# Output and FFN left factors built from rows kept in SBUF at written units, and the gate pair's weight sums ordered behind the softmax heads

## The chip, the core and the metric

The kernel runs on one core of a Trainium2 chip. TensorE (PE) multiplies matrices into PSUM, its weight loads (PEld) overlap the multiplications; VectorE (DVE), ScalarE (ACT) and GpSimd (POOL) do the elementwise work; SyncE (SP) issues nearly all DMA transfers between DRAM and SBUF. Each engine takes its instructions in the order in which the compiled program has them; semaphores order them across engines. The metric is the device time of one execution in microseconds, here the median of several timed runs; less is better.

## What is computed

One decoder layer on 512 tokens of width 2048, all in float32 (`reference`, cut):

```python
h = rms_norm(x, norm1_g[l])
proj = h @ w_in[l]
qa, ka, va, ra, ga, qb, kb, vb = jnp.split(proj, split_points, axis=-1)
log_g = jax.nn.log_sigmoid(ga @ gla_gate_w2[l] + gla_gate_b[l]) / GLA_GATE_TAU
out_a = gla_mixer(qa, ka, va, ra, log_g, onorm_g)      # 4 heads, ends with  * silu(ra)
out_b = dilated_mixer(rms_norm(qb), rms_norm(kb), vb, rel_bias)   # 8 softmax heads
mix = jnp.concatenate([out_a, out_b], axis=-1)
x = x + mix @ w_out[l]
h2 = rms_norm(x, norm2_g[l])
x = x + (jax.nn.silu(h2 @ w_gate[l]) * (h2 @ w_up[l])) @ w_down[l]
```

Nearly all arithmetic is in five matrix products with `w_in`, `w_out`, `w_gate`, `w_up` and `w_down` (2048 to 5632 wide).

## The kernel before

**Products.** Each large product is done with one level of Strassen's scheme (the Winograd form): the left factor (activations, transposed) and the weights are cut into quarters, and seven products P1 to P7 of sums of quarters replace eight. A left sum is called A11, S1, S2, S4, S3, A12 or A22 and belongs to P1, P5, P6, P3, P7, P2 or P4 in that order, which is the order in which they run. Float32 accuracy is had by splitting every factor into a high and a low part: the high part is a cast on ScalarE, the low part a subtraction on VectorE, and three of the four products of parts are taken.

**Pairs and units.** Class `Pair` stands for two column blocks of 512 columns that share a left factor. `stream` walks through the pairs. A pair has 7 products times 4 groups of rows: 28 units, and a unit is one weight quarter of 128x1024 elements with 12 matmuls (line 358): eight with the weight's high part, four with its low part. For unit k the loop does in this order: the high part of the weight of unit k+1 on ScalarE (line 331), the weight sum of unit k+2 on VectorE (`total`, which calls `Pair.source`, line 256; P5, P6, P7 and P4 need one), the low part of unit k+1 on VectorE (line 335), eight matmuls, then `p.step()`, then four matmuls. P5 subtracts quarter a from b, P6 a from d, P7 b from d, P4 a from c, each time into the second one's buffer.

**Left factors.** Class `Operand` holds the split left sums. `split` makes one from a row tile: a cast on ScalarE (line 161), a subtraction of 512 columns on VectorE (line 162), into a buffer of the pool `apool` (28 buffers). The left factor of the output projection (`opm`) has rows of the softmax heads as its upper half (`mix_d[4]` to `mix_d[7]`) and rows of the GLA heads as its lower half (`mix_d[0]` to `mix_d[3]`); that of the FFN (`opn`) is made of the normed output (`xn_d`). In the kernel before, all these rows are stored to DRAM when they have been turned (`transposed_store`, TensorE transposes at line 1019, ScalarE copies at lines 1027 and 1030, store at line 1034) and fetched again whenever a sum needs them (`part`, line 1073, and `fetch_part`, line 1107).

**Order.** `step` first runs what was put off with `later(units, ...)` and then takes one step of the first generator in `background`; `rate` and `paced` say at which units a step is taken. In the gate pair (columns 2048 and 2560 of the input projection, the last pair over `opx`) 0.72 steps a unit are taken: `dil_heads(4)` and `dil_heads(6)`, two softmax heads at a time in eight steps each, then `early_job` for A11 and S3 of `opm`; what isn't made when the output pair begins is made there at once (`finish`). During the output pair `late_jobs` makes the rest, one sum and split per unit, with loads one item ahead. For the FFN's left factor `operand_jobs` builds groups 0 and 1 during the second output pair, and `early_job` and `late_jobs` groups 2 and 3 at the beginning of the first FFN pair.

A step of a softmax head (`scores`) is: one score matmul (line 904), an add with a running minimum on VectorE (line 907), an exponential on ScalarE (line 910), a reciprocal (line 913) and a multiplication on VectorE (line 914).

The first pair alone is ordered by hand (`PLAN`). For the rest, a list scheduler of the framework orders each engine's instructions when the program is compiled; an instruction whose inputs it holds to be ready may be put far ahead of its place in the text. `tc.issue_after(ins)` adds an edge: what is traced inside the block comes after `ins` on that engine.

Of the kernel before, what the change touches and what calls it, by code (L numbers as in the profile page):

```python
# [18 lines left out]
P = 128  # L19
# [6 lines left out]
NB = 640  # L26
PRODUCTS = ("P1", "P5", "P6", "P3", "P7", "P2", "P4")
# [69 lines left out]
def block_kernel(ctx: ExitStack, tc: tile.TileContext, ins, out):  # L97
# [138 lines left out]
    class Pair:  # L236


        def __init__(self, op, rows, w1, w2, final, step, scale=None, before=None):
            self.op, self.rows, self.w1, self.w2 = op, rows, w1, w2  # L240
            self.final, self.step, self.scale, self.before = final, step, scale, before
            self.q, self.dst, self.held = {}, {}, {}

# [6 lines left out]
        def source(self, prod, g):  # L250

            if prod in SINGLE:
                return self.quarter(SINGLE[prod], g)
            one, two = SUMS_OF[prod]
            src = self.quarter(two, g)
            nc.vector.tensor_tensor(src, self.quarter(one, g), src, op=ALU.subtract)  # L256
            return src
# [608 lines left out]
    def dil_head(h, lane):  # L866
# [34 lines left out]
        def scores(b):  # L901
# [5 lines left out]
            nc.vector.tensor_tensor_reduce(  # L907
                lg[:, :n], lp[:, :n], tb[:, 512 - n :], -1.0, 3.0e38, ALU.add, ALU.min, st[:, 0:1]
            )
# [4 lines left out]
            nc.vector.tensor_scalar(lg[:, :n], lg[:, :n], st[:, 3:4], None, op0=ALU.mult)  # L914
# [51 lines left out]
    def in_turn(*gens):  # L966
        for g in gens:
            yield from g


    def heads_norm(t):
# [4 lines left out]
        for h in range(4):  # L976
# [35 lines left out]
    def transposed_store(tiles, half, dsts, gains=None, spare=None):  # L1012

        for b in range(2):
# [7 lines left out]
            if spare is None:  # L1022
                d = work(("oT", "PT")[b], (P, 2, 256))
            else:
                d = spare[:, b]
            if gains is None:
                nc.scalar.copy(d, bk)
            else:
                for jj in range(2):
# [3 lines left out]
                    )  # L1033
            store(dsts[b][half], d)
            done.add((id(dsts[b]), half))

    def final_gate(half, which, tiles, acc_):
# [11 lines left out]
        for m in range(2):  # L1049
# [27 lines left out]

    def early_job(op, wanted, flip):
        h0, h1 = (1, 0) if flip else (0, 1)
        return op.early([(g, part(top, h0), part(top, h1)) for g, top in wanted])  # L1080
# [31 lines left out]
    def late_jobs(op, groups, tops, bots, flip):  # L1112

        h0, h1 = (1, 0) if flip else (0, 1)
        tt = nc.vector.tensor_tensor
        sums = {}

        def sum_of(name, g, op1):
            def use(t):
                if name == "S1":  # L1120
                    tt(sums[g], t, sums[g], op=ALU.add)
                elif name == "S2":
                    tt(sums[g], sums[g], t, op=ALU.subtract)
                else:
                    tt(sums[g], t, sums[g], op=ALU.subtract)
                op.split(name, g, sums[g])

            return use

        def both(g):  # L1130
            fetch = fetch_part(tops[g], h1)[1]

            def get():
                sums[g] = part(bots[g], h1)()
                return fetch()

            return (id(bots[g]), h1), get

        items = []
        for part_ in groups:  # L1140
            for g in part_:
                items.append((*both(g), sum_of("S1", g, op)))
            for g in part_:
                items.append((*fetch_part(tops[g], h0), sum_of("S2", g, op)))
        groups = [g for part_ in groups for g in part_]
        for g in groups:
            items.append((*fetch_part(bots[g], h0), sum_of("S4", g, op)))
        for name, half in (("A12", h0), ("A22", h1)):
            for g in groups:
                items.append(  # L1150
                    (*fetch_part(bots[g], half), lambda t, name=name, g=g: op.split(name, g, t))
                )
        return staged(items)
# [22 lines left out]
    pair(opx, rows_in, col(2048), col(2560), final_gate, rate((27, 0.72), (1, 0)), row_scale)  # L1176
# [23 lines left out]

    def final_out(second):
        def final(half, which, tiles, acc_):
# [31 lines left out]
    def output_scales(part):  # L1234
# [6 lines left out]
        else:  # L1241
# [7 lines left out]
    pair(opm, rows_mix, ocol(0), ocol(512), final_out(0), paced([1] * 28),  # L1249
         before=lambda: finish(lambda: ("S3", 3) in opm.t))  # L1250
# [181 lines left out]
```

## Time and profile before

| | |
|---|---|
| median of three timed runs | 1965.07 us (1964.33 to 1965.67) |
| profiled execution, device time | 1958.01 us |
| its span, first to last instruction | 1956.1 us |
| TensorE clock granted | 0.999 |
| DMA packets, bytes moved | 158855, 362.52 MB |
| read from and written to DRAM | 298.68 MB and 64.51 MB |

A profile is one execution as the hardware recorded it. Times are in us from the first instruction. A line such as "L335 DVE TENSOR_TENSOR wl<-wa,wh ... x376 | 458.7, 1223" names the source line, the engine, the operation, what it writes and reads, how often, the busy time and the mean duration of one in ns. A bracket such as "[3.91 <-DMA v<-mix_d]" in the timeline is idle time of the engine before an instruction and what ended it. The chain of waits is followed back from the last instruction: at each step to what released it. In windows, each engine has its busy time and, after x, its number of instructions. Matmul ends are modelled, so TensorE shown as busy isn't always at its full pace; counts times the pace tell more.

### The profile page before, as it was taken

What the parts mean: (1) busy time and instruction counts of PE and PEld (TensorE: products, weight loads), DVE (VectorE), ACT (ScalarE), POOL (GpSimd) and SP (SyncE); (2) the same over time, 40 slices, a digit from 0 to 9 for tenths busy, and PEclk for the clock granted to TensorE, in tenths of its full rate; (3) what the DMA queues carried; (4) which work ended last, traced back from release to release, by engine and by line L of the source; (5) the groups of instructions that cost most, each with busy time, mean ns of one, the idle gap of its engine ahead of it and who ended that gap; (6) DMA issues with size and microseconds to landing.
All of it is one profiled execution on the core that took longest, in us unless ns stands there. A gap on an engine that the chain in (4) does not pass through costs nothing.

```text
span 1956.1 us, 25599 instructions
## 1 busy us (share of the span) xinstructions
PE 1918.2 (98%) x9160; PEld 1657.3 (85%) x9160; DVE 1648.0 (84%) x1845; ACT 1088.1 (56%) x1580; POOL 55.2 (3%) x73
## 2 busy tenths in 40 slices
PE   8999999999999999999999999999999999999998
PEld 6788888888878888888888888888888888888887
DVE  7996887768789989878878879879879989989977
ACT  9654554667666665544544545545546646546443
POOL 0000330011000000000000000000000000000000
PEclk9999999999999999999999999999999999999999
DMA  9545555444567584453453453443445865855662
GB/s 355 174 154 206 179 173 171 143 156 162 198 217 241 181 289 148 154 188 141 155 183 135 162 182 120 171 171 124 173 170 176 279 212 182 292 198 180 230 215 76
DMA packets 158855, 362.52 MB, mean 185 GB/s; under 512 B 16438, under 2 KB 43359, under 8 KB 158728
## 3 DMA queue, kind: packets, MB, share of 16 engines
q1 hardware_dynamic: 158584, 360.89, 53.1%
q8 instruction: 71, 1.16, 0.2%
q14 instruction: 56, 0.46, 0.1%
q10 hardware_dynamic: 144, 0.01, 0.0%
HBM read 298.68 MB, written 64.51 MB: 186 GB/s over the span
## 4 chain that ended last, share of the span: by engine, by line
PE 75%; DVE 6%; DMA 3%; issue 2%; ACT 1%; SPq 0%; POOL 0%; DVEq 0%; ACTq 0%
PE acc L358 71%; DVE wl L335 2%; PE bank L1019 1%; DVE wa L256 1%; PE bank L926 1%; PE bank L904 1%; DVE AS L162 1%; PE bank L919 0%; DMA xn_d<-PT 0%; DMA q<-y_d 0%; PE bank L895 0%; DMA q<-in_x 0%; DMA T<-p_d 0%; DMA r<-xn_d 0%; ACT wh L331 0%
## 5 line engine op out<-in xcount | busy, mean ns | idle before, releaser
L358 PE MATMUL acc<-wh,AS 128*128 128x512 f32 x3008 | 712.2, 379 | 0.9 <-DVE AS L162 0.8
L358 PEld LDWEIGHTS acc<-wh,AS 128*128 128x128 f32 x3008 | 568.0, 189 | 82.8 <-DVE AS L162 1.6
L331 ACT CAST wh<-wa 128x1024 fp32r<-128x1024 f32 x376 | 394.3, 1049 | 395.1 <-PE acc L358 365.2
L358 PE MATMUL acc<-wh,AA 128*128 128x512 f32 x2256 | 533.7, 379 | 1.1 <-ACT wh L331 0.9
L335 DVE TENSOR_TENSOR wl<-wa,wh 128x1024 fp32r<-128x1024 f32 x376 | 458.7, 1223 | 74.5 <-ACT wh L331 45.6
L358 PEld LDWEIGHTS acc<-wh,AA 128*128 128x128 f32 x2256 | 426.0, 189 | 62.7 <-ACT wh L331 2.3
L358 PE MATMUL acc<-wl,AS 128*128 128x512 f32 x1504 | 395.3, 385 | 7.6 <-DVE wl L335 7.5
L358 PEld LDWEIGHTS acc<-wl,AS 128*128 128x128 f32 x1504 | 279.2, 189 | 61.0 <-DVE wl L335 20.3
L358 PE MATMUL acc<-wl,AA 128*128 128x512 f32 x1128 | 296.1, 385 | 3.4 <-DVE wl L335 3.3
L358 PEld LDWEIGHTS acc<-wl,AA 128*128 128x128 f32 x1128 | 209.3, 189 | 35.8 <-DVE wl L335 7.5
L331 ACT CAST wh<-wb 128x1024 fp32r<-128x1024 f32 x94 | 98.6, 1049 | 123.8 <-PE acc L358 117.1
L331 ACT CAST wh<-wc 128x1024 fp32r<-128x1024 f32 x94 | 98.4, 1047 | 109.2 <-PE acc L358 106.6
L331 ACT CAST wh<-wd 128x1024 fp32r<-128x1024 f32 x94 | 98.6, 1049 | 103.6 <-PE acc L358 98.5
L335 DVE TENSOR_TENSOR wl<-wc,wh 128x1024 fp32r<-128x1024 f32 x94 | 115.0, 1223 | 41.7 <-ACT wh L331 41.7
L335 DVE TENSOR_TENSOR wl<-wd,wh 128x1024 fp32r<-128x1024 f32 x94 | 114.8, 1223 | 37.8 <-ACT wh L331 28.7
L256 DVE TENSOR_TENSOR wa<-wc,wa 128x1024 f32<-128x1024 f32 x94 | 114.8, 1225 | 35.6 <-DMA wc<-in_w_gate 20.8
L335 DVE TENSOR_TENSOR wl<-wb,wh 128x1024 fp32r<-128x1024 f32 x94 | 114.5, 1221 | 5.3 <-ACT wh L331 4.9
L256 DVE TENSOR_TENSOR wa<-wb,wa 128x1024 f32<-128x1024 f32 x94 | 113.8, 1222 | 1.7 <-DMA wb<-in_w_in 1.0
L256 DVE TENSOR_TENSOR wb<-wd,wb 128x1024 f32<-128x1024 f32 x94 | 114.8, 1223 | 0.4
L256 DVE TENSOR_TENSOR wa<-wd,wa 128x1024 f32<-128x1024 f32 x94 | 113.5, 1223 | 0.1
L298 DVE SCALAR_TENSOR_TENSOR seed<-acc,rs,seed 128x512 f32<-128x512 f32 x96 | 70.5, 747 | 27.6 <-PE acc L358 27.5
L282 ACT ACTIVATE seed<-acc,rs 128x512 f32<-128x512 f32 x96 | 60.8, 682 | 3.1 <-PE acc L358 3.1
(285 smaller groups left out, 1332.2 us busy)
## 6 DMA issues: line engine op xcount, KB each, us to landing
wa<-in_w_gate SPq DMA_DIRECT2D x44, 512.0 KB, 3.4
wb<-in_w_up SPq DMA_DIRECT2D x44, 512.0 KB, 4.0
wd<-in_w_up SPq DMA_DIRECT2D x44, 512.0 KB, 4.1
wc<-in_w_gate SPq DMA_DIRECT2D x44, 512.0 KB, 3.4
wc<-in_w_in SPq DMA_DIRECT2D x28, 512.0 KB, 3.5
wa<-in_w_in SPq DMA_DIRECT2D x24, 512.0 KB, 4.9
wb<-in_w_in SPq DMA_DIRECT2D x24, 512.0 KB, 5.7
wd<-in_w_in SPq DMA_DIRECT2D x24, 512.0 KB, 5.1
```

Source lines behind the costliest of these rows:

```text
L162: nc.vector.tensor_tensor(a[:, :, 1, :], src, a[:, :, 0, :].bitcast(F32), op=ALU.subtract)
L256: nc.vector.tensor_tensor(src, self.quarter(one, g), src, op=ALU.subtract)
L282: nc.scalar.activation(halves(t), unfolded(src[m]), AF.Copy, scale=self.scale(half, m))
L298: nc.vector.scalar_tensor_tensor(halves(seed[m]), unfolded(src[m]), self.scale(half, m), halves(seed[m]), op0=ALU.mult, op1=ALU.add,)
L331: nc.scalar.copy(high[k], sources[k])
L335: nc.vector.tensor_tensor(low[k], sources.pop(k), high[k].bitcast(F32), op=ALU.subtract)
L358: nc.tensor.matmul(p.dst[prod][m], a[:, jj, hl, m * P : (m + 1) * P], folded(w[:, jj, :]), start=fresh and g == 0 and len(terms) == 2 and ...
L904: nc.tensor.matmul(lp[:, :n], qh[:, b * P : (b + 1) * P], kh[:, :n], start=True, stop=True)
L926: nc.tensor.matmul(op, vh[:, k, :], lgs[b][:, k * P : (k + 1) * P], start=(k == 0), stop=(k == b))
L1019: nc.tensor.transpose(bk[:, jj, m * P : (m + 1) * P], tiles[m][:, f : f + P], ident)
```

## The change

- A table `GATE` says at which unit of the gate pair, and `OUT` at which unit of the first output pair, each fetch, sum and split of `opm` is traced (`scripted`, `mixed`). "T.g" fetches both halves of the top row of group g into one buffer; "2.g" makes the sums of S1 and S2. `early_job` and `late_jobs` are gone, and so are the stores of the turned GLA rows: `transposed_store` without `dsts` leaves them in `spare`, and `kept` remembers the tiles.
- For the FFN, the second output pair's turned rows stay in SBUF too (`kept_n`). `kept_job` makes groups 2 and 3 from them, in the order of `KEPT`, one word a step, and waits while a row isn't there. Groups 0 and 1 still go through DRAM. The turn of the last quarter of each output pair is put off by two units instead of three, and the first FFN pair has another list of steps.
- In the gate pair (`hold=True`) each weight sum is traced inside `issue_after` of the latest VectorE instruction of the softmax heads (`recent["head"]`, set at lines 907 and 914).

```diff
+KEPT = "A11.2 A11.3 =S3.2+S3.2 =S3.3+S3.3 =S2.2+=S1.2+S1.2 =S2.3+=S1.3+S1.3 S2.2 S2.3 =S4.2+S4.2 =S4.3+S4.3 A12.2 A12.3 A22.2 A22.3"
+GATE = {
+    9: "T.0 T.1", 11: "A11.0", 12: "S3.0", 13: "A11.1", 14: "S3.1", 16: "T.2", 18: "A11.2", 19: "S3.2",
+    21: "2.0 S1.0", 22: "2.1", 23: "S1.1", 24: "S2.0", 25: "T.3 S2.1", 27: "A11.3",
+}
+OUT = {
+    0: "S3.3", 2: "2.2 S1.2", 3: "2.3 S1.3", 4: "S2.2", 5: "S2.3", 9: "S4.0", 10: "S4.1", 11: "S4.2", 12: "S4.3",
+    17: "A12.0 A12.1", 18: "A12.2", 19: "A12.3", 21: "A22.0", 22: "A22.1", 24: "A22.2", 25: "A22.3",
+}
...
             src = self.quarter(two, g)
-            nc.vector.tensor_tensor(src, self.quarter(one, g), src, op=ALU.subtract)
+            other = self.quarter(one, g)
+            with ExitStack() as behind:
+                if self.hold and "head" in recent:
+                    behind.enter_context(tc.issue_after(recent["head"]))
+                nc.vector.tensor_tensor(src, other, src, op=ALU.subtract)
...
         "qb1": lambda: [
             dil_heads(4),
-            together(dil_heads(6), in_turn(*(early_job(opm, [(g, mix_d[4 + g])], True) for g in range(3)))),
-            early_job(opm, [(3, mix_d[7])], True),
-            late_jobs(opm, ((0, 1), (2, 3)), mix_d[4:], [mix_d[b] for b in order], True),
+            dil_heads(6),
         ],
...
+            if dsts is None:
+                continue
             store(dsts[b][half], d)
...
-        spare = apool.tile([P, 2, 2, 256], F32, name=nm("turned"), tag="A")
-        later(2, lambda: transposed_store(
-            tiles, half, mix_d[2 * which : 2 * which + 2], spare=spare
-        ))
+        def turn():
+            if which == 1:
+                t = apool.tile([P, 2, 2, 256], F32, name=nm("turned"), tag="A")
+                spare = [t[:, 0], t[:, 1]]
+            else:
+                spare = [work(n, (P, 2, 256)) for n in (("qT", "kT"), ("v", "T"))[half]]
+            transposed_store(tiles, half, None, spare=spare)
+            for b in range(2):
+                kept[2 * (which == 0) + b, "r" + str(1 - half)] = spare[b]
+
+        later(2, turn)
...
+    def mixed(name, g):
+        g = int(g)
         tt = nc.vector.tensor_tensor
+        if name == "T":
+            t = apool.tile([P, 2, 2, 256], F32, name=nm("top"), tag="A")
+            for i in range(2):
+                kept[g, "t" + str(i)] = part(mix_d[4 + g], 1 - i)(t[:, i])
+            return
+        t0, t1 = kept[g, "t0"], kept[g, "t1"]
+        if name == "A11":
+            opm.split(name, g, t0)
+        elif name == "S3":
+            tt(t1, t0, t1, op=ALU.subtract)
+            opm.split(name, g, t1)
+        elif name == "2":
+            tt(t1, kept[g, "r1"], t1, op=ALU.subtract)
+            tt(t0, t1, t0, op=ALU.add)
+        elif name == "S1":
+            opm.split(name, g, t0)
+        elif name == "S2":
+            opm.split(name, g, t1)
+        elif name == "S4":
+            tt(t1, kept[g, "r0"], t1, op=ALU.subtract)
+            opm.split(name, g, t1)
+        else:
+            opm.split(name, g, kept[g, "r0" if name == "A12" else "r1"])
...
-    pair(opx, rows_in, col(2048), col(2560), final_gate, rate((27, 0.72), (1, 0)), row_scale)
+    pair(opx, rows_in, col(2048), col(2560), final_gate, scripted(rate((27, 0.72), (1, 0)), GATE), row_scale, hold=True)
...
+    def kept_job(op, kept):
...
+        for word in KEPT.split():
+            for one in word.split("+"):
...
+                while not all(have(n) for n in needs):
+                    yield
...
+            yield
...
             def turn():
-                transposed_store(tiles, tok, dsts, gains)
-                if not second and which == 0 and half == 1:
-                    background.append(operand_jobs(opn, tops, bots, 0, 2))
-                elif second and which == 1 and half == 1:
-                    background.append(early_job(opn, [(g, tops[g]) for g in (2, 3)], False))
-                    background.append(late_jobs(opn, ((2, 3),), tops, bots, False))
-
-            later(3 if which == 0 and half == 1 else 2, turn)
+                if not second:
+                    transposed_store(tiles, tok, dsts, gains)
+                    if which == 0 and half == 1:
+                        background.append(operand_jobs(opn, tops, bots, 0, 2))
+                        background.append(kept_job(opn, kept_n))
+                    return
...
+                transposed_store(tiles, tok, None, gains, spare=kept_n["tr"[which == 0], tok])
+
+            later(2, turn)
...
-    pair(opm, rows_mix, ocol(0), ocol(512), final_out(0), paced([1] * 28),
-         before=lambda: finish(lambda: ("S3", 3) in opm.t))
+    pair(opm, rows_mix, ocol(0), ocol(512), final_out(0), scripted(step, OUT))
...
-    paces = {0: [0, 1, 1, 1, 1, 0, 0, 1, 1] + [0] * 6, 10: [0] * 6}
+    paces = {0: [1, 1, 1, 1, 0, 0, 0, 0, 0, 0, 1, 1, 1, 1, 0, 0, 0, 0], 10: [0] * 6}
     def before_ffn(j):
         if j == 0:
-            finish(lambda: ("S3", 3) in opn.t)
+            finish(lambda: ("A11", 3) in opn.t)
```

More of the change, by code (lines that the diff above doesn't have):

```diff
@@ L26 @@
 NB = 640
+KEPT = "A11.2 A11.3 =S3.2+S3.2 =S3.3+S3.3 =S2.2+=S1.2+S1.2 =S2.3+=S1.3+S1.3 S2.2 S2.3 =S4.2+S4.2 =S4.3+S4.3 A12.2 A12.3 A22.2 A22.3"
+GATE = {
+    9: "T.0 T.1",
+    11: "A11.0",
+    12: "S3.0",
+    13: "A11.1",
+    14: "S3.1",
+    16: "T.2",
+    18: "A11.2",
+    19: "S3.2",
+    21: "2.0 S1.0",
+    22: "2.1",
+    23: "S1.1",
+    24: "S2.0",
+    25: "T.3 S2.1",
+    27: "A11.3",
+}
+OUT = {
+    0: "S3.3",
+    2: "2.2 S1.2",
+    3: "2.3 S1.3",
+    4: "S2.2",
+    5: "S2.3",
+    9: "S4.0",
+    10: "S4.1",
+    11: "S4.2",
+    12: "S4.3",
+    17: "A12.0 A12.1",
+    18: "A12.2",
+    19: "A12.3",
+    21: "A22.0",
+    22: "A22.1",
+    24: "A22.2",
+    25: "A22.3",
+}
 PRODUCTS = ("P1", "P5", "P6", "P3", "P7", "P2", "P4")
@@ L236, in block_kernel, with __init__ @@
     class Pair:
-        def __init__(self, op, rows, w1, w2, final, step, scale=None, before=None):
+        def __init__(self, op, rows, w1, w2, final, step, scale=None, before=None, hold=False):
             self.op, self.rows, self.w1, self.w2 = op, rows, w1, w2
@@ L242, in __init__ @@
             self.q, self.dst, self.held = {}, {}, {}
+            self.hold = hold
         def quarter(self, name, g):
@@ L1110, in fetch_part @@
         return (id(src), half), fetch
-    def late_jobs(op, groups, tops, bots, flip):
-        h0, h1 = (1, 0) if flip else (0, 1)
-        tt = nc.vector.tensor_tensor
[L1116 to L1153, printed above, removed]
@@ new lines, in block_kernel, with scripted, go @@
+    kept = {}
+    def scripted(pace, script):
+        k = [0]
+        def go():
+            pace()
+            for word in script.get(k[0], "").split():
+                mixed(*word.split("."))
+            k[0] += 1
+        return go
+    def mixed(name, g):
+        g = int(g)
+        tt = nc.vector.tensor_tensor
+        if name == "T":
[21 more added lines that the diff above has]
+            opm.split(name, g, kept[g, "r0" if name == "A12" else "r1"])
```

38 lines of the change are left out of this document (31 added, 7 removed).

## The prediction, made before the changed kernel ran

> **What bounds the kernel now.** I read the first part of the page, then the chain of waits, then windows cut where one weight quarter ends and the next begins.
>
> ```profile
> span 1956.1 us, 25599 instructions
> PE 1918.2 (98%) x9160; PEld 1657.3 (85%) x9160; DVE 1648.0 (84%) x1845; ACT 1088.1 (56%) x1580; POOL 55.2 (3%) x73
> ```
>
> TensorE sets the time, and the change adds and removes none of its 9160 matmuls. So the only time to be won is what TensorE spends below its own pace. The pace stands in the chain, where it is alone:
>
> ```profile
> 346.10 5.18 PE acc L358 x24
> 618.07 0.87 PE bank L1019 x8
> ```
>
> One product matmul takes 5.18/24 = 0.216 us and one transpose 0.87/8 = 0.109. A unit (one weight quarter, 12 matmuls) needs 2.59 us. Twenty-eight units are a pair. The change touches the last pair of the input projection (gate pair, from 453 us), the two pairs of the output projection (from 558.54 and from about 642) and the first FFN pair (from about 720). The windows, first of all instructions, then of the product matmuls alone (the count under PEld is exact):
>
> ```profile
> 548.96:558.54 9.58, 8.48 (x40) 6.82 (x38) 9.25 (x13) 6.12 (x10) 0.00 (x0) 1.00 0.86 309
> 558.54:595.46 36.92, 32.56 (x147) 25.46 (x146) 36.92 (x45) 25.15 (x37) 0.00 (x0) 1.00 0.38 129
> 653.36:681.52 28.16, 27.41 (x121) 22.03 (x120) 28.16 (x33) 18.62 (x29) 0.00 (x0) 1.00 0.31 103
> 717.07:757.07 40.00, 34.47 (x161) 28.31 (x160) 35.26 (x45) 26.82 (x45) 0.00 (x0) 1.00 0.58 195
> 756.00:1500.00 744.00, 743.89 (x3523) 650.80 (x3524) 610.55 (x593) 378.53 (x434) 0.00 (x0) 1.00 0.45 159
> ...
> 548.96:558.54 9.58, 8.29 (x38) 6.65 (x36) 1.00 0.86 309
> 558.54:595.46 36.92, 31.32 (x133) 24.08 (x132) 1.00 0.38 129
> 653.36:681.52 28.16, 27.41 (x121) 22.03 (x120) 1.00 0.31 103
> 717.07:757.07 40.00, 33.21 (x145) 26.50 (x144) 1.00 0.58 195
> ```
>
> Columns: length, then busy time and count of PE, PEld, DVE, ACT, POOL, then clock and DMA. Window by window, length minus matmuls times 0.216 minus transposes times 0.109:
>
> - end of the gate pair: 9.58 - 36 x 0.216 - 2 x 0.109 = 1.6 us lost
> - first eleven units of the output projection: 36.92 - 132 x 0.216 - 14 x 0.109 = 6.9 lost, VectorE busy for 36.92 of 36.92
> - 653.36 to 681.52: 28.16 - 120 x 0.216 = 2.3 lost, VectorE full again
> - start of the FFN: 40.00 - 144 x 0.216 - 16 x 0.109 = 7.2 lost, and here VectorE is not full
>
> Together 18.0 us: the ceiling of what the change can give. Behind 756 us TensorE is busy in 743.89 of 744.00, so a stall that is removed earlier isn't found again there.
>
> Two kinds of cause are visible. The first is VectorE having too much to do; the second is VectorE and ScalarE, which work in order, standing before a row that has gone to DRAM and back:
>
> ```profile
> 548.31 0.69 DVE L1121 TENSOR_TENSOR r<-v,r 128x512 f32<-128x512 f32 x1 [3.91 <-DMA v<-mix_d]
> 719.18 0.62 ACT L161 CAST AA<-top 128x512 fp32r<-128x512 f32 x1 [4.26 <-DMA top<-xn_d]
> 719.25 0.69 DVE L215 TENSOR_TENSOR top<-top 128x512 f32<-128x512 f32 x1 [3.08 <-DMA top<-xn_d]
> 722.42 0.69 DVE L215 TENSOR_TENSOR top<-top 128x512 f32<-128x512 f32 x1 [1.87 <-DMA top<-xn_d]
> ...
> 710.30 7.00 DMA xn_d<-PT
> 719.15 5.35 DMA q<-in_x
> 729.97 5.05 DMA r<-xn_d
> ```
>
> The last three come from the chain of waits. While SyncE waits for the store of 7.00 us before it may load those rows, the residual load q<-in_x behind it in the queue doesn't start either.
>
> **The change part by part.**
>
> Output rows kept (turned GLA rows, old stores of line 1034 and loads of lines 1107 and 1073). Removed: 8 stores and 24 loads of 256 KB (six fetches in each of four groups). The four top rows are still fetched, as eight loads now issued at written units. VectorE's arithmetic is equal: four sums and seven splits in each group before and after, the S1 and S2 sums only built another way round. Price of one, with the wide ones beside it:
>
> ```profile
> 559.42 1.22 DVE wa L256
> 560.64 1.14 DVE wl L335
> 563.51 1.21 DVE AS L162 x2
> ...
> 509.72:595.46 85.74, 79.86 (x397) 65.82 (x396) 74.76 (x115) 60.22 (x107) 0.00 (x0) 1.00 0.58 199
> 490.31:513.17 22.86, 22.86 (x135) 20.75 (x134) 12.47 (x11) 12.85 (x19) 0.00 (x0) 1.00 0.53 181
> ```
>
> A sum or split of 512 columns takes 1.21/2 = 0.60 us, a weight sum or low part of 1024 columns 1.14 behind another. The transfers themselves lie beside TensorE work; they cost where an engine stands before them. Gone is the 3.91 us of VectorE at 548, which comes just before the stretch in which VectorE never catches up.
>
> Ledger of VectorE from 509.72 to 595.46 (13 units of the gate pair, 11 of the output projection). TensorE needs 85.74 - 1.6 - 6.9 = 77.2. VectorE was busy for 74.8 there and idle for 11.0. Row operations that the scripts place there: in the gate pair A11.2, S3.2 (2), the S1 and S2 sums of two groups (4), S1.0, S1.1, S2.0, S2.1, A11.3, that is 12; in the output pair up to unit 10 S3.3 (2), two groups of S1 and S2 (8), S4.0 and S4.1 (4), that is 14. Before, the splits of line 162 stood there 14 times by these windows of that line alone (the third is used further down), with twelve sums: 26 too.
>
> ```profile
> 509.72:558.54 48.82, 2.06 (x3) 1.00 0.72 252
> 558.54:595.46 36.92, 7.38 (x11) 1.00 0.38 129
> 717.07:757.07 40.00, 6.71 (x10) 1.00 0.58 195
> ```
>
> The rows, then, move no work out of the stretch; five of these operations (3.0 us) go from its dense half to the half with the idle time (14 instead of 19 stay behind 558.54).
>
> The hold (source, with hold=True in the gate pair alone). It adds no instruction, but each weight sum now goes behind the last multiplication of the heads traced so far. What it forbids stands here; these ran long before their use:
>
> ```profile
> 484.14 1.22 DVE L256 TENSOR_TENSOR wb<-wd,wb 128x1024 f32<-128x1024 f32 x1
> ...
> 501.62 1.22 DVE L256 TENSOR_TENSOR wa<-wc,wa 128x1024 f32<-128x1024 f32 x1
> ...
> 508.55 1.22 DVE L256 TENSOR_TENSOR wa<-wc,wa 128x1024 f32<-128x1024 f32 x1
> ...
> 515.71 0.28 DVE L914 TENSOR_SCALAR PT<-PT,mx 128x128 f32<-128x128 f32 x1
> ...
> 520.13 0.34 DVE L914 TENSOR_SCALAR r<-r,mx 128x256 f32<-128x256 f32 x1
> ...
> 533.41 0.48 DVE L914 TENSOR_SCALAR r<-r,mx 128x512 f32<-128x512 f32 x1
> ```
>
> The sums of P4 (wa<-wc) are traced at units 20 to 23 of the gate pair, when the last heads' step is the one whose multiplication ran at 533.41. Three of them (501.62, 505.99, 508.55; the fourth ran at 512.03, inside the ledger) leave a stretch in which VectorE was busy for 12.47 of 22.86 and enter the full one. So do two of P7 (wb<-wd), which go behind the steps at 515.71 and 520.13. Five times 1.14 = +5.7. The ledger is then 74.8 + 5.7 = 80.5 against 77.2 of TensorE: 3.3 us short, at best 0 (one P7 sum of the output pair and S4.0, S4.1, 3.5 us in all, aren't due before the stretch ends), at worst 7 (waiting for scores, about 3.5 of idle time that stays, comes on top). I take 3.3, as VectorE stood full in the dense rows above. Lost 8.5 before, 3.3 after: **-5.2** (bounds -8.5 and -1.5).
>
> What else the hold touches: the six sums of P5 to P7 that now follow a heads' step directly. Queued behind a waiting sum are the low part of the weights (line 335) and so TensorE. The sum behind 520.13 belongs to the unit whose first matmul stands fourth in the twelve below, at 523.71 + 3 x 0.216 = 524.4:
>
> ```profile
> 523.71 2.59 PE acc L358 x12
> ...
> L331 ACT CAST wh<-wa 128x1024 fp32r<-128x1024 f32 x376 | 394.3, 1049 | 395.1 <-PE acc L358 365.2
> ```
>
> The multiplication ends at 520.4; 1.14 for the sum and 1.05 for the high part on ScalarE make 522.6, so 1.8 us to spare. I put it at **0**; with the cover gone it is the rival below.
>
> 653.36 to 681.52: the first two FFN groups still go through DRAM (operand_jobs), with as many operations; their start comes a unit earlier. **0** (bounds -1 and +1.5: the earlier transposes could wait for the residual).
>
> FFN start (kept_job, groups 2 and 3). Removed: 8 stores and 16 loads; with them the waits of 4.26, 3.08 and 1.87, the 7.00 before which SyncE stood, and the row that lands 5.05 after 729.97. Of the eighteen 512-column operations that stood between 717 and 757 (ten splits by the window above, eight sums), twelve stay (three each at the pair's last unit and the next, then 1, 1, 2 and 2): 35.3 - 6 x 0.60 = 31.6 of VectorE against 40.0 - 7.2 = 32.8 of TensorE, so it fits. The six that go earlier fall into this stretch, whose VectorE has 3.9 us free:
>
> ```profile
> 681.52:717.07 35.55, 35.55 (x173) 30.98 (x172) 31.64 (x36) 21.96 (x37) 0.00 (x0) 1.00 0.83 284
> ```
>
> Late next is the turn of the last output quarter, now two units after its close instead of three: it needs q<-in_x, which no longer queues behind the row loads. I leave 1.0 us for it: 7.2 to 1.0 = **-6.2** (bounds -7.2 and -3).
>
> [...]
>
> Sum: -5.2 + 0 + 0 - 6.2 = -11.4. The profiled execution took 1958.0 us (span 1956.1 and 1.9 around it), so 1946.6. The median of the timed runs is 1965.1, 7.1 above it; the same difference gives **1953.7 us**.
>
> **The rivals.**
>
> A. The hold starves TensorE (slower). Place: units 3 to 19 of the gate pair, six heads' steps. A sum waits in order for scores, exponential and multiplication of the second head; by the rows one such chain is
>
> ```profile
> 487.77 0.69 DVE L907 CUSTOM_DVE_ANT_0 r<-bank,r 128x512 f32<-128x512 f32 x1 [0.60 <-PE bank L904]
> 490.31 0.49 DVE L914 TENSOR_SCALAR r<-r,mx 128x512 f32<-128x512 f32 x1
> ```
>
> from 487.77 to 490.80, 3.0 us. Were none of it covered, 6 x 3.0 = 18 us are lost, and 1965.1 - 11.4 + 18 = 1972. It decides from 11.4/6 = 1.9 us a step on. For it: the sums ran early for a reason. Against: 1.8 us to spare even at the tightest step, and the heads' chains themselves get shorter without sums between. Chance 0.13.
>
> B. The ledger is right, but the dense stretch doesn't give: the moved sums take what the scripts win (bound -1.5), and the FFN start gives half (-3.6): -5, 1960. Chance 0.18.
>
> C. No change: the transfers were hidden and VectorE alone sets the pace in all four stretches, so that each lost time comes back as VectorE time. For it: 36.92 of 36.92. Against: the FFN start, with VectorE at 35.26 of 40.00 and named DMA waits of 4.3 and 4.9. 1964 (within 2). Chance 0.10. [...]
>
> D. All comes back, also in 653 to 681: -8.5 - 1 - 7.2 = -16.7, 1948. Chance 0.12.
>
> **How the numbers follow.** The forecast (-7 to -14) has 0.47. What one can tell from no change is 0.2%, 3.9 us. Faster beyond it: forecast 0.47, D 0.12, most of B 0.16, together 0.75. Slower beyond it: nearly all of A, 0.12. Same: the rest, 0.13. The range leaves out A above (0.13) and some of D below (0.05): 1946 to 1966; the forecast's own is 1951 to 1958.
>
> **What would show it.** In the gate pair: no weight sum before its heads' multiplication, and wa<-wc after about 533; if TensorE then waits for line 335 in units 3 to 19, A is right. No wait for mix_d but the tops; none for xn_d after 700 us. The output pair's first eleven units should last 30 to 33.5 us instead of 36.9, and the stretch from the FFN's first unit on 33 to 35 instead of 40. VectorE still full in the first with the same length means C. I'd be wrong if the first window stays long while VectorE is idle in it: then a kept row or a late T load stands in front.

## The result, and the profile after

The changed kernel takes 1952.76 us (median of four runs, 1947.99 to 1954.0) where the kernel before took 1965.02 in four (1964.33 to 1965.67). The ratio is 0.9933 with a 95% interval of 0.9919 to 0.9947, so it is faster by 0.5 to 0.8%. The profiled execution took 1952.11 us.

First the page of the changed kernel, its head and its transfers:

```profile
span 1950.0 us, 25512 instructions
PE 1916.9 (98%) x9160; PEld 1660.6 (85%) x9160; DVE 1647.6 (84%) x1845; ACT 1088.9 (56%) x1580; POOL 47.2 (2%) x73
...
DMA packets 150791, 347.84 MB, mean 178 GB/s; under 512 B 15542, under 2 KB 42463, under 8 KB 150664
```

TensorE and VectorE have as many instructions as before and, within 1.3 us, as many busy microseconds; only transfers went (14.7 MB). So whatever was won was waiting time. Windows of the changed kernel, cut at the same units as the prediction's (ten units of the gate pair; its last three; the first eleven of the output projection; the twelve at the FFN's start; what follows). The columns are the prediction's:

```profile
514.67:554.80 40.13, 39.04 (x214) 33.58 (x213) 39.32 (x71) 29.86 (x63) 0.00 (x0) 1.00 0.52 163
554.80:564.08 9.28, 9.01 (x46) 7.58 (x44) 9.10 (x14) 7.85 (x13) 0.00 (x0) 1.00 1.01 387
564.08:595.03 30.95, 30.34 (x142) 25.41 (x140) 30.95 (x35) 21.27 (x31) 0.00 (x0) 1.00 0.04 14
715.25:749.31 34.06, 33.23 (x161) 28.71 (x160) 33.57 (x43) 24.28 (x41) 0.00 (x0) 1.00 0.17 64
749.31:1494.00 744.69, 744.11 (x3524) 650.58 (x3523) 609.94 (x592) 379.15 (x435) 0.00 (x0) 1.00 0.49 159
```

The output projection's first eleven units last 30.95 us instead of 36.92, the FFN's start 34.06 instead of 40.00. Behind it TensorE is busy for 744.11 of 744.69, as before, so nothing was put off to there. VectorE still is full in the first (30.95 of 30.95), but with 35 instructions in place of 45. Which ones left shows in the groups of VectorE's instructions in that stretch, before (busy, mean ns, idle before):

```profile
L162 DVE TENSOR_TENSOR AS<-r,AS 128x512 fp32r<-128x512 f32 x9 | 6.2, 697 | 0.0
...
L1123 DVE TENSOR_TENSOR r<-r,kT 128x512 f32<-128x512 f32 x2 | 1.4, 700 | 0.0
L1123 DVE TENSOR_TENSOR r<-r,qT 128x512 f32<-128x512 f32 x2 | 1.4, 696 | 0.0
...
L1125 DVE TENSOR_TENSOR r<-T,r 128x512 f32<-128x512 f32 x1 | 0.7, 703 | 0.0
L1125 DVE TENSOR_TENSOR r<-v,r 128x512 f32<-128x512 f32 x1 | 0.7, 701 | 0.0
L1121 DVE TENSOR_TENSOR r<-T,r 128x512 f32<-128x512 f32 x1 | 0.7, 698 | 0.0
L1121 DVE TENSOR_TENSOR r<-v,r 128x512 f32<-128x512 f32 x1 | 0.7, 697 | 0.0
L162 DVE TENSOR_TENSOR AA<-top,AA 128x512 fp32r<-128x512 f32 x1 | 0.7, 689 | 0.0
L162 DVE TENSOR_TENSOR AS<-top,AS 128x512 fp32r<-128x512 f32 x1 | 0.7, 689 | 0.0
```

and after:

```profile
L197 DVE TENSOR_TENSOR AS<-top,AS 128x512 fp32r<-128x512 f32 x6 | 4.0, 677 | 0.0
...
L1187 DVE TENSOR_TENSOR top<-top 128x512 f32<-128x512 f32 x2 | 1.4, 680 | 0.0
L197 DVE TENSOR_TENSOR AA<-top,AA 128x512 fp32r<-128x512 f32 x1 | 0.7, 681 | 0.0
L1186 DVE TENSOR_TENSOR top<-qT,top 128x512 f32<-128x512 f32 x1 | 0.7, 681 | 0.0
L1186 DVE TENSOR_TENSOR top<-kT,top 128x512 f32<-128x512 f32 x1 | 0.7, 679 | 0.0
L1193 DVE TENSOR_TENSOR top<-turned,top 128x512 f32<-128x512 f32 x1 | 0.7, 675 | 0.0
```

Eleven splits and eight sums became seven and five: seven row operations of 0.60 us, 4.2 us, are no longer in this stretch. The other three of the ten are one low part of a weight, one weight sum (wb<-wd) and one addition of line 1062 (1104 after). At the FFN's start the cause is another. The waits there, before (who waited, for whom; us in total, times, longest):

```profile
PEld acc L358 <- DVE wl L335: 7.6, 6, 2.2
PE acc L358 <- DVE wl L335: 5.4, 5, 1.8
DVE top L215 <- DMA top<-xn_d: 4.9, 2, 3.1
ACT AA L161 <- DMA top<-xn_d: 4.5, 2, 4.3
```

and after:

```profile
PEld acc L398 <- DVE wl L375: 1.5, 2, 1.2
...
PE acc L398 <- DVE wl L375: 0.8, 1, 0.8
...
DVE q L1237 <- DMA q<-in_x: 0.5, 1, 0.5
```

Read from the bottom up. Before, VectorE and ScalarE stood 9.4 us for rows on their way through DRAM, and TensorE stood behind the low parts that VectorE was then late with. After, no row is waited for, VectorE is busy for 33.57 of 34.06, and TensorE's waits for it fall from 5.4 to 0.8 (those of its weight loads, PEld, from 7.6 to 1.5).

### The profile page after: what moved, and what is told of

It is laid out like the page before. It is cut to its first block, busy times and chain, and to the rows that moved or that the text cites. A ratio compares the mean times of both kernels' runs of the same rounds, so it can differ in the third digit from the quotient of the medians.

```text
span 1950.0 us, 25512 instructions
## 1 busy us (share of the span) xinstructions
PE 1916.9 (98%) x9160; PEld 1660.6 (85%) x9160; DVE 1647.6 (84%) x1845; ACT 1088.9 (56%) x1580; POOL 47.2 (2%) x73
## 4 chain that ended last, share of the span: by engine, by line
PE 72%; DVE 7%; DMA 3%; issue 2%; ACT 1%; SPq 0%; POOLq 0%; POOL 0%; DVEq 0%; ACTq 0%
PE acc L398 68%; DVE wl L375 3%; PE bank L1059 1%; DVE wa L296 1%; PE bank L944 1%; PE bank L968 1%; DVE AS L197 1%; DMA wc<-in_w_in 0%; DMA p_d<-PT 0%; PE bank L935 0%; PE bank L961 0%; ACT wh L371 0%; DMA r<-p_d 0%; ACT jk L1019 0%; DMA q<-in_x 0%
## 5 line engine op out<-in xcount | busy, mean ns | idle before, releaser
L398 PEld LDWEIGHTS acc<-wl,AS 128*128 128x128 f32 x1504 | 280.1, 189 | 55.4 <-DVE wl L375 13.6
```

The costliest lines, as they stand in the source:

```text
L398: nc.tensor.matmul(p.dst[prod][m], a[:, jj, hl, m * P : (m + 1) * P], folded(w[:, jj, :]), start=fresh and g == 0 and len(terms) == 2 and ...
```

## The experiments

**How the runs are compared.** Besides the ratio of times, each profiled execution gives TensorE's loss by stretch: length, minus matmuls times 0.216, minus transposes times 0.109 (scores by their columns), as in the prediction. Units are counted from the gate pair's first: 28 to a pair, so gate pair 0 to 27, output pairs 28 to 55 and 56 to 83, FFN from 84. The expectations count from the first unit of the whole stream, which gives numbers larger by 112: their unit 116 is unit 4 here, their 127 to 136 are 15 to 24. "Clock" is the part of the loss that goes with a granted clock of 0.50: 1.7 us for each stretch of 3.41 us, half of its length; the windows stand at the end.

| run | unit 4 | 15 to 24 | 25 to 38 | 60 to 69 | 83 to 94 | units 0 to 94 | of it clock | ratio to before |
|---|---|---|---|---|---|---|---|---|
| before | 2.6 | 0.7 | 8.5 | 2.3 | 7.2 | 22.0 | 0 | |
| b_again | 3.0 | 0.9 | 8.8 | 2.6 | 7.6 | 24.0 | 0 | 1.0007 (0.9998 to 1.0017) |
| after | 5.2 | 1.6 | 2.2 | 0.8 | 1.2 | 12.0 | 1.7 | 0.9933 (0.9919 to 0.9947) |
| after_again | 5.4 | 0.9 | 2.2 | 0.8 | 0.7 | 10.8 | 1.7 | 0.9949 (0.9933 to 0.9965) |
| hold_only | 4.6 | 0.4 | 7.2 | 1.3 | 6.3 | 21.7 | 1.7 | 0.9993 (0.9983 to 1.0002) |
| ffn_only | 2.8 | 0.9 | 7.5 | 2.3 | 1.2 | 15.4 | 0 | 0.9959 (0.9944 to 0.9974) |
| rows_only | 2.8 | 2.3 | 1.7 | 1.0 | 6.9 | 15.3 | 1.7 | 0.9951 (0.9931 to 0.9970) |
| no_hold | 3.9 | 4.1 | 1.7 | 1.0 | 0.7 | 12.3 | 3.4 | 0.9954 (0.9939 to 0.9969) |
| hold_late | 4.8 | 0.9 | 2.2 | 0.7 | 0.7 | 10.2 | 1.7 | 0.9938 (0.9921 to 0.9954) |
| t2_early | 5.3 | 1.0 | 2.3 | 0.4 | 0.7 | 10.5 | 1.7 | 0.9943 (0.9928 to 0.9959) |
| stores_back | 5.2 | 0.9 | 3.8 | 1.3 | 1.5 | 13.6 | 1.7 | 0.9937 (0.9922 to 0.9952) |
| late_heads | 3.1 | 0.2 | 5.0 | 0.4 | 0.7 | 10.0 | 1.7 | 0.9938 (0.9926 to 0.9951) |
| late_heads_no_hold | 2.9 | 0.3 | 1.5 | 0.7 | 1.1 | 7.6 | 0 | 0.9925 (0.9910 to 0.9939) |
| before_late_heads | 2.3 | 0.1 | 8.5 | 0.9 | 7.8 | 20.5 | 0 | 0.9991 (0.9982 to 1.0000) |

Each ratio stands against the kernel before, run beside it. Its median was 1965.02 us beside the changed kernel and 1962.07, 1962.14 and 1960.55 in the three groups of later runs.

**What a repeat does.** The kernel before once more, and later the changed one.

> The kernel before once more, for a second trace of it. If the 7 us between its profiled execution (1958.0) and its timed runs (1965) lie in single places, a second trace loses about 36 us of TensorE time in all with other places than the first. If they are the granted clock, the units keep their losses and all are some 0.3% longer.

> The changed kernel once more, on the chip of its variants, for a second trace. Units 112 to 206 of the stream should lose 12.0 us again (22.0 before), with about 5 of them at unit 116; the ratio 0.992 to 0.995.

The same program gave 1.0007 against itself. Its trace has a span of 1961.1 us instead of 1956.1, with 2.0 of the 5.0 in the stretch of the table and 3.0 outside. So a single span says little below 5 us; a loss in one stretch repeats within about 1. Where the spread between executions comes from is taken up at the end. The change repeats: 0.9949 (0.9933 to 0.9965), with 10.8 lost instead of 12.0.

**The parts alone.** The changed kernel without the hold:

```diff
-    pair(opx, rows_in, col(2048), col(2560), final_gate, scripted(rate((27, 0.72), (1, 0)), GATE), row_scale, hold=True)
+    pair(opx, rows_in, col(2048), col(2560), final_gate, scripted(rate((27, 0.72), (1, 0)), GATE), row_scale)
```

> The changed kernel without the hold; all else is kept. By the ledger of the prediction the hold puts five weight sums (5.7 us of VectorE) into the stretch where VectorE is full, so without it that stretch (units 127 to 150 of the stream, 3.9 us lost in the changed kernel) should lose 0 to 2 us: 1949 to 1952. The rival, that the hold keeps the heads' steps and with them TensorE going, expects more loss in the gate pair without it: 1955 to 1958.

The kernel before with the hold alone (excerpt):

```diff
+            other = self.quarter(one, g)
+            with ExitStack() as behind:
+                if self.hold and "head" in recent:
+                    behind.enter_context(tc.issue_after(recent["head"]))
+                nc.vector.tensor_tensor(src, other, src, op=ALU.subtract)
...
-    pair(opx, rows_in, col(2048), col(2560), final_gate, rate((27, 0.72), (1, 0)), row_scale)
+    pair(opx, rows_in, col(2048), col(2560), final_gate, rate((27, 0.72), (1, 0)), row_scale, hold=True)
```

> The kernel before with the hold alone. By the ledger: five sums more in the full stretch, 8.5 us lost there become 11 to 14, in all 1967 to 1970. The rival expects 1960 to 1964.

The kernel before with the FFN's rows kept (kept_job, KEPT, its turn and step list), the output projection as it was (excerpt):

```diff
+                        background.append(kept_job(opn, kept_n))
...
-            later(3 if which == 0 and half == 1 else 2, turn)
+            later(2, turn)
...
-    paces = {0: [0, 1, 1, 1, 1, 0, 0, 1, 1] + [0] * 6, 10: [0] * 6}
+    paces = {0: [1, 1, 1, 1, 0, 0, 0, 0, 0, 0, 1, 1, 1, 1, 0, 0, 0, 0], 10: [0] * 6}
```

> The kernel before with the FFN's rows kept in SBUF alone (kept_job, the turns after two units, the new list of steps). The prediction gave this part -6.2 us: 1958 to 1960, with the window at the FFN's start down from 7.2 us lost to about 1. If the rows were hidden behind VectorE's work: 1964 to 1966.

And the changed kernel with neither hold nor kept FFN rows (the FFN's part, its step list and the turn after three units as before), so that only the output projection's rows are kept, at the written units (excerpt):

```diff
-                        background.append(kept_job(opn, kept_n))
...
+                    background.append(early_job(opn, [(g, tops[g]) for g in (2, 3)], False))
+                    background.append(late_jobs(opn, ((2, 3),), tops, bots, False))
```

> The output projection's rows kept with the written units, without the hold and with the FFN's part as before. If the parts add up (FFN -7, hold about -1), 1958 to 1960; units 140 to 150 lose about 1.6 (6.9 before), units 127 to 136 about 4 (0.8 before) and unit 116 about 3.9, units 195 to 206 about 7. If the prediction's ledger is right that rows alone win 8 us from unit 127 on: 1954 to 1956.

The two halves of the gain separate by column. Kept output rows alone take units 25 to 38 from 8.5 to 1.7 us and leave the FFN's start at 6.9 (of it 1.7 by the half clock); kept FFN rows alone take the FFN's start from 7.2 to 1.2 and leave 7.5 at the output projection. Each is worth some 0.4 to 0.5% in time, but the times don't add up: 0.9959 times 0.9951 is 0.9910, and both parts together without the hold gave 0.9954 (0.9939 to 0.9969). In the table they win 6.6 and 6.7 us alone and 9.7 together. Of the missing 3.6, 1.7 is that no_hold has one half-clock stretch more than rows_only; the times miss about 7, and why that much is open. The expectations were reckoned from 1965 us, and the kernel before stands 3 lower in these runs. With 3 us added, hold_only (1961.01) and no_hold (1953.13) fall where their rivals had them and not where the prediction's ledger did, ffn_only (1954.69) just under its forecast and rows_only (1953.62) between its two. The hold alone can't be told from nothing (0.9993), and the changed kernel without it (0.9954) can't be told from the one with it (0.9933 and 0.9949). At the output projection keeping the rows and tracing them at written units came in one edit; no run has one without the other.

What the hold does is seen on VectorE. The sums of P4 and two of P7 in the changed kernel's timeline:

```profile
520.79 1.22 DVE L296 TENSOR_TENSOR wb<-wd,wb 128x1024 f32<-128x1024 f32 x1
...
525.65 1.22 DVE L296 TENSOR_TENSOR wb<-wd,wb 128x1024 f32<-128x1024 f32 x1
...
543.22 1.22 DVE L296 TENSOR_TENSOR wa<-wc,wa 128x1024 f32<-128x1024 f32 x1
...
547.90 2.35 DVE L296 TENSOR_TENSOR wa<-wc,wa 128x1024 f32<-128x1024 f32 x2
...
551.30 1.21 DVE L296 TENSOR_TENSOR wa<-wc,wa 128x1024 f32<-128x1024 f32 x1
```

They went where the prediction put them. Without the hold, one of them stands in front of a heads' step that is ready, and TensorE then waits for that step's multiplication (timeline of no_hold, VectorE and then TensorE):

```profile
518.46 1.22 DVE L296 TENSOR_TENSOR wa<-wc,wa 128x1024 f32<-128x1024 f32 x1
519.59 0.28 DVE L947 CUSTOM_DVE_ANT_0 L<-bank,T 128x128 f32<-128x128 f32 x1
...
522.35 0.30 PE L961 MATMUL bank<-mats,L 128*128 128x128 f32 x1 [2.05 <-DVE L L954]
```

That is most of the 4.1 in its row: 2.05 of waiting and 1.7 of half clock behind it (0.51 from 523.42 to 526.83 us). So the hold wins at units 15 to 24 once the rows are kept and the heads' steps are in their old place (0.9 to 1.6 with it, 2.3 and 4.1 without); in the kernel before there is next to nothing to win there (0.7 and 0.4). It loses at unit 4, where all six runs with the hold and the heads' steps in their old place have 4.6 to 5.4 and the five without it 2.6 to 3.9. TensorE's timeline there, changed kernel:

```profile
467.69 0.38 PE L398 MATMUL acc<-wl,AS 128*128 128x512 f32 x1
471.54 0.66 PE L935 MATMUL bank<-mats,q 128*128 128x128 f32 x4 [3.47 <-DMA q<-qb]
```

and the kernel before:

```profile
465.78 0.91 PE L358 MATMUL acc<-wl,AS 128*128 128x512 f32 x3
468.24 0.66 PE L895 MATMUL bank<-mats,q 128*128 128x128 f32 x4 [1.54 <-DMA q<-qb]
```

With the hold, one low matmul (x1) stands ahead of the heads' transposes in TensorE's order; without it there are three (x3). It is so in every run of the table. TensorE takes its work in that order, so in front of the same load q<-qb it has 2 x 0.216 = 0.43 us less to do. That accounts for hold_only, where it stands 2.06. In the changed kernel the load also lands later, though it is issued 12.3 us after the gate pair's first unit, as in the kernel before and in no_hold (12.2): the first transpose comes 15.94 us after that unit, against 14.87 before and 15.07 in no_hold.

**Which sums the hold is for.** Only P7 and P4 held, the heads' first sums left free:

```diff
-                if self.hold and "head" in recent:
+                if self.hold and prod in ("P7", "P4") and "head" in recent:
```

> The changed kernel with the hold on the sums of P7 and P4 alone. If the hold costs at the pair's beginning (unit 116, through the sums of P5 and P6) and wins later (units 127 to 136, through P7 and P4), unit 116 loses 3.9 as without the hold and units 127 to 136 lose 1.6 as with it: 1 us less than the changed kernel. If it is one whole, there is no difference.

The load lands earlier again (15.17 us after the gate pair's first unit) and the wait for it shrinks from 3.47 to 2.17 us, so holding the sums of P5 and P6 does delay it in the changed kernel. It doesn't in the kernel before (15.13 in hold_only), and by which link it does here wasn't followed. But the order with one low matmul stays, and so does the half clock behind the stall (0.50 from 471.0 to 474.0 us); waits of 0.27 and 0.37 come beside it, and unit 4 loses 4.8 instead of 5.2. The time, 0.9938, can't be told from that of the changed kernel.

**The wait for a top row.** VectorE's timeline of the changed kernel has one long wait left in the gate pair, for the third top row:

```profile
514.46 0.69 DVE L1183 TENSOR_TENSOR top<-top 128x512 f32<-128x512 f32 x1 [5.07 <-DMA top<-mix_d]
```

Its load three units earlier:

```diff
-    13: "A11.1",
+    13: "A11.1 T.2",
...
-    16: "T.2",
```

> The changed kernel with T.2 traced at unit 13 instead of 16. VectorE's wait of 5.07 us for top<-mix_d at 514 us should go; with it up to 1 us of the 1.6 lost in units 127 to 136. If that wait was covered, no difference.

The same wait in that kernel's timeline:

```profile
513.38 0.69 DVE L1182 TENSOR_TENSOR top<-top 128x512 f32<-128x512 f32 x1 [3.87 <-DMA top<-mix_d]
```

It shrank by 1.2 us only, and the columns stayed (1.0 and 2.3). TensorE lost 0.7 in units 5 to 14 with the longer wait and with the shorter: it is covered there. As the wait didn't vanish, its price where it isn't covered was not measured.

**The heads one unit later.** To get q<-qb landed before TensorE stands for it, one empty step is put between the fetch of heads 4 and 5 and their next step, in the changed kernel, without its hold, and in the kernel before:

```diff
+            if _ == 0 and h == 4:
+                yield
```

> The changed kernel with one empty step between the fetch of softmax heads 4 and 5 and their transposes. With the hold TensorE's order puts the sixteen transposes of unit 116 after one low matmul instead of three, and it stands there until the fetch has landed. One step later (about 1.4 units, 3.6 us) the fetch should be there: unit 116 loses under 1 us instead of 5, in all 3 to 5 us less than the changed kernel. The rival: the later heads run into the sums of the gate pair's end and units 127 to 151 give the gain back; no difference.

> The same without the hold. If the hold is worth its time once unit 116 no longer pays for it, this loses 2 us more than late_heads in units 127 to 136. If not, the two are equal.

> The kernel before with the same empty step. Unit 116 loses 2.6 to 3.0 us there for the same reason: with the step 0 to 1, in all 1 to 3 us faster than before, if the dense stretch from unit 137 on does not take it back.

The edit didn't do at unit 4 what it was meant for. TensorE's timeline of late_heads, there and at the end of the gate pair:

```profile
468.85 0.48 PE L398 MATMUL acc<-wl,AS 128*128 128x512 f32 x1 [0.27 <-DVE wl L375]
471.69 0.66 PE L935 MATMUL bank<-mats,q 128*128 128x128 f32 x4 [2.36 <-DMA q<-qb]
...
560.74 0.30 PE L1061 MATMUL bank<-mats,seed 128*128 128x128 f32 x1 [1.83 <-DVE seed L1106]
```

In all three runs the compiled order has the transposes where they were without the step, behind the 57th product matmul of the gate pair with the hold and behind the 59th without. TensorE still stands for the load there (2.36, 1.84 and 1.75 us); what moved is the score matmuls behind the transposes. So unit 4 didn't fall under 1 us. That it falls from 5.2 to 3.1 with the hold is a shorter wait (the load landed 0.6 us sooner after the pair's first unit) and no half clock (1.00 from 469.78 to 476.60 us). And a stall comes up at the end of the gate pair: VectorE had just stood 1.31 us for the load og<-ong_d and was late with the rows that TensorE transposes here. The 1.83 of waiting and 1.7 of half clock (0.51 from 561.95 to 565.36 us) take the gain away again. Only this trace has the stall, and none of those with the hold alone or the later heads alone; by which link the two make it wasn't followed. Without the hold: 7.6 us lost in all, the least of any run, and 0.9925 (0.9910 to 0.9939), the lowest ratio. Of the 4.7 less than in no_hold, 1.7 is the half clock at unit 4, where TensorE stood for the load as long as in no_hold (1.84 and 1.74 us) and the granted clock stayed at 1.00. At units 15 to 24 it loses no more than late_heads (0.3 and 0.2), so with the later heads the hold wins nothing there. Its interval overlaps those of late_heads and stores_back on the same chip, so it is the best version seen but not shown to beat the changed kernel. In the kernel before the same step is worth at most 0.2% (0.9991).

**Transfers or waiting?** The sixteen stores that the change took out are made again, and nothing reads them:

```diff
-            transposed_store(tiles, half, None, spare=spare)
+            transposed_store(tiles, half, mix_d[2 * which : 2 * which + 2], spare=spare)
...
-                transposed_store(tiles, tok, None, gains, spare=kept_n["tr"[which == 0], tok])
+                transposed_store(tiles, tok, dsts, gains, spare=kept_n["tr"[which == 0], tok])
```

> The changed kernel with the sixteen stores of turned rows put back; nobody reads them. If the gain came from the waits for rows, the losses stay: 11 to 12 us in units 112 to 206. If it came from fewer transfers: units 137 to 150 and 195 to 206 lose 2 to 4 us more together.

The losses rise from 2.2 to 3.8 and from 1.2 to 1.5, of some 6 us won in each place, and the time (0.9937) doesn't show it. So at most about a quarter of what was won came from fewer stores. These are 16 of the 56 transfers that the change took out; the 40 loads weren't put back, and what fewer loads are worth apart from the waits for them was not measured.

## Why the prediction was right

1953.7 us were predicted and 1952.76 measured, by the terms as follows.

- **The ceiling.** 18.0 us in four places. Three of the four fell to 0.6 (units 25 to 27), 1.6 (28 to 38) and 0.8 (60 to 69), the fourth to 1.2: 18.0 to 4.3.
- **Output rows and VectorE's ledger, -5.2.** Over units 15 to 38 the loss went from 9.2 to 3.9, that is -5.4, and the stretch lasts 80.36 us where the ledger had 80.5. The size is right; its parts were not, so that the two agree this closely is in part luck. Seven row operations left the dense half, not five. And the +5.7 for the hold is no price: VectorE was busy for 39.32 + 9.10 + 30.95 = 79.4 us with the hold, and in no_hold for 74.10, as the sum under these windows of its own says (the column of VectorE is the third pair):

```profile
514.30:556.85 42.55, 40.50 (x214) 34.72 (x212) 34.37 (x67) 29.75 (x63) 0.00 (x0) 0.96 0.52 173
556.85:565.62 8.77, 8.77 (x45) 7.58 (x44) 8.77 (x13) 7.75 (x13) 0.00 (x0) 1.00 0.81 278
565.62:596.58 30.96, 30.35 (x141) 25.41 (x140) 30.96 (x36) 21.27 (x31) 0.00 (x0) 1.00 0.03 12
```

  With 5.3 us less to do there TensorE lost 5.8, of it 1.7 by the clock, so 4.1 against 3.9. The ledger treated the whole stretch as one sum of work against time. But by the prediction's own rows VectorE was busy in the ten gate units for 74.76 - 9.25 - 36.92 = 28.6 us of 85.74 - 9.58 - 36.92 = 39.2, so 10.7 were free ahead of the dense half. The moved sums went into that, and the dense half was relieved by the rows alone: it lost 1.6 with the hold and without.
- **The hold's other sums, 0.** Wrong at one place. Unit 4 lost 5.2 instead of 2.6. The prediction asked whether a held sum is late for TensorE; what happened is that TensorE's own order changed. The four runs that differ in the hold alone agree: before against hold_only 2.6 and 4.6, no_hold against changed 3.9 and 5.2. Rival A had the place but neither the mechanism nor the price (2 us, not 18), and what the hold wins at units 15 to 24 pays for it.
- **653 to 681, 0.** It went from 2.3 to 0.8, outside the bound of -1. before_late_heads has 0.9 there with the operations of the kernel before, ffn_only 2.3 with the FFN's operations of the changed one. So it isn't the change's operations but how the low parts happen to fall among the others on a full VectorE. Why they fell better was not settled.
- **FFN start, -6.2.** Measured 7.2 to 1.2, and 0.7 in the repeat: right. But sixteen of the eighteen row operations stayed in the stretch, not twelve (nine splits and seven sums of lines 197 and 1268), so VectorE had 33.6 us of work, not 31.6. It just fits in the 34.06. The 1.0 left for the late residual was nearly right: 0.5 of waiting for q<-in_x.
- **The last step, from the profiled execution to the median.** The sum came to 1946.6 for a profiled execution, and it took 1952.1. In units 0 to 94 it lost 10.0 less than before (11.4 were forecast), but outside of them the span was 3.9 longer, as the repeat of the kernel before was by 3.0. The 7.1 from the profiled execution up to the median was 0.65 this time. These two errors, 5.5 and 6.4, nearly cancel, so that the time came out within 0.9 us is luck. What bears the forecast out is the change itself: -11.4 against -12.3 of the medians, and -10 to -16 by the ratio's interval; the repeat has -9.2 of the medians.
- **The rivals.** B and C fall with the two columns that emptied (2.2 and 1.2). C's ground, that VectorE sets the pace where it is full and each lost time comes back, fails at the output projection: VectorE was full before and after, but ten of its instructions went elsewhere. D was right that 653 to 681 comes back too; of its 16.7 us 12.9 came (5.4, 1.5 and 6.0), nearer to the forecast's 11.4, and it had neither unit 4 nor the rest of the span.

The runs that speak for the mechanism are rows_only and ffn_only with their disjoint columns, and stores_back, which brings the stores back and not the waiting. Not separated are the kept rows from the written units at the output projection, and the loads from the waits for them.

## What to carry to other kernels

An engine that works in order can stand for a row's way through DRAM even when its total work would fit (9.4 us of VectorE and ScalarE at the FFN's start, with VectorE busy for 35.26 of 40.00); keep the row, and the units behind it get their low parts in time (TensorE's waits for them fell from 5.4 to 0.8 us). Where one engine is full for a stretch and idle before it (in the kernel before 36.92 of 36.92 us behind 28.6 of 39.2), move the work across that border rather than taking it away, and count its instructions on each side. An edge that only orders one engine can change another engine's compiled order as well (one low matmul in front of the load q<-qb instead of three): look at the unit in front of each load, not only at the instructions that were held. And a step that is moved in the text need not move in the compiled order (the transposes stayed behind the 57th and the 59th product matmul): look there before reading the result.

## What the hardware showed that was not expected

Behind some stalls of TensorE the granted clock was at half for 3.41 us. Windows of that length in the changed kernel, TensorE alone (busy and count, granted clock, DMA share, GB/s), around the stall at unit 4:

```profile
469.28:472.69 3.41, 1.15 (x11) 1.00 0.49 143
472.69:476.10 3.41, 3.41 (x15) 0.50 0.00 0
```

In no_hold, around its two stalls:

```profile
468.81:472.22 3.41, 1.65 (x10) 1.00 0.54 155
472.22:475.63 3.41, 3.27 (x15) 0.51 0.00 1
520.01:523.42 3.41, 1.36 (x9) 1.00 0.63 215
523.42:526.83 3.41, 3.41 (x9) 0.51 0.58 205
```

And in rows_only, one stall without the effect and one with it:

```profile
467.66:471.07 3.41, 1.53 (x10) 1.00 0.54 156
471.07:474.48 3.41, 3.27 (x23) 1.00 0.00 0
733.91:737.32 3.41, 1.52 (x8) 1.00 0.51 161
737.32:740.73 3.41, 3.41 (x10) 0.51 0.82 297
```

From 440 to 770 us nine of the runs have ten such stretches, each of 3.41 or 3.42 us by windows of 0.5 us. In the four windows above that were followed by half clock, TensorE worked for 1.65 us or less of 3.41; over the next 3.41 us the granted clock was 0.50 or 0.51, and half of that length is 1.71 us. This is the whole difference between the 3.47 us of idle time and the 5.2 lost at unit 4 of the changed kernel. Idle time alone doesn't tell which stall is followed by half clock: in rows_only 1.5 of the 3.4 us were busy both in the window from 733.91 (1.89 idle, and the clock fell) and in that from 467.66 (1.88 idle, and it didn't); the clock of no_hold fell after 1.76, that of late_heads didn't after 1.91 (469.78 to 473.19 us). What decides it was not shown. Half clock is also why no_hold lost more at unit 4 (3.9, with 1.76 idle in its window) than rows_only (2.8, with 1.88).

This also answers in part what b_again was made for. In 39 executions of the kernel before on one chip the median time is 1959.6 us at a granted clock of 1.000, 1961.3 at 0.999, 1962.0 at 0.998 and 1964.9 at 0.997. Reckoned from the windows above, 3.41 us of half clock take 0.0009 off the mean clock of such an execution and cost 1.71 us, so the 5.3 us between the first and the last of these are about three such stretches: an estimate from these numbers. So much of the spread between executions of one program would fit with how many half-clock stretches each of them has, and a profiled execution is one draw of it; in the others they were not counted.
